# Eighteen convolution taps a layer moved from VectorE to ScalarE products and accumulating transfers, and VectorE's remaining taps placed anew

## The chip, the cores and the metric

The kernel runs on one core of a Trainium2 chip. The metric is the device time of one execution in microseconds. The kernel before takes 1769.1 us, the median of three runs (1768.19 to 1769.87).

## What is computed

The reference is a trunk of two layers (sequence 512, width 1024). Each layer feeds three mixers with one projection of the normed input, gates them per channel, and goes on to a feed-forward and an embedding:

```python
h = rmsnorm(x, norm_mix[i])
qa, ka, va, glu_in, qc, kc, vc, gates = jnp.split(h @ w_in[i], SPLITS, axis=-1)
ya = diff_attention(qa, ka, va, ...)          # 4 heads, two softmaxes a head
yb = conformer_conv(glu_in, ...)              # the part that the change touches
yc = neighbourhood_attention(qc, kc, vc, rpb) # 8 heads on an 8 x 64 grid
ga, gb, gc = jnp.split(jax.nn.sigmoid(gates), 3, axis=-1)
merged = ga * (ya @ w_br_a) + gb * (yb @ w_br_b) + gc * (yc @ w_br_c)
x = x + merged @ w_o[i]
...                                           # feed-forward, gated embedding
```

The convolution module is a gated unit `z = a * sigmoid(g)`, then a depthwise convolution over the sequence with 31 taps for each of 512 channels, a bias, a layer norm and a silu. A depthwise tap is a product of a shifted row with one number per channel, and a sum.

## The kernel before

**Engines.** All matrix products are on TensorE (PE), in pairs of high and low parts: each weight block of 128x1024 is loaded by SyncE's queue (SP) into a tile `wr`, ScalarE (ACT) copies it to `wh`, VectorE (DVE) subtracts to get `wl` (`split`, called by `weights`, lines 166 to 177). Activations are split in the same way. PE's order is the order of the program text; the other engines' instructions are placed by a scheduler from priorities and dependencies.

**Order of a layer** (`layer`, from line 432). Names in the profile begin with the stage: `glu` (three of the four blocks of the gated unit), `natten` (neighbourhood attention: `natten_in` for queries and keys of two heads at a time, `natten_v` for the values, whose four sums stand in PSUM as two `natten_mm`, a `natten_av` and a `natten_sc`), the last gated block, `diff` (differential attention: `diff_in` for each of four heads, `diff_v` for the values) with `gatec` (eight blocks of gate c, one after `diff_in(1)`, seven after `diff_in(3)`), `gateb`, `branchc`, `mergea`, more `gateb`, the convolution's norm (`conv`), `mergeb`, `wo`, the feed-forward `ffn`, and `ple`. Attention units (scores, softmax, values) are generators; a counter of PE's chunks starts them some chunks after their inputs, and runs their later steps, so that they lie between the blocks of other stages.

**Softmax steps that the prediction uses.** In a neighbourhood unit PE writes scores to a PSUM tile `natten_sc` (L722; two buffers, shared with the value sum of that name and with `diff_sc`), VectorE takes the minimum (L726), ScalarE the exponential. In a differential unit VectorE takes the maximum (L919), ScalarE writes the exponentials `diff_a` and `diff_e`. At the end of a head ScalarE scales the output (`diff_t`), GpSimd (POOL) raises the mean square to a power (`diff_rc`, L227, inside `norm`), and PE transposes that column (`diff_tr`, L231).

**The taps.** 31 taps for each of four filters j (128 channels each) are steps of VectorE over the whole sequence, 124 a layer: the first a product plus bias (L549), the others a product plus the sum so far (L164, `conv_z<-glu_z,pre_par,conv_z`). They are one generator, `taps`, drawn in order of j and then of tap by `background(act, n)`: it takes the next n taps and lets each follow a given step of the stage. A table of numbers, `BG` (line 49), says how many a step of each stage draws; what is left at the norm is drawn there (`conv`).

**Tiles.** `z` has 5 buffers (gated inputs and sums), `t` has 7 (temporary tiles of 128x512 for all stages), `b` has 2 (biases of neighbourhood units, later quarters of the feed-forward's activations).

**GpSimd** has little else in this part of the program: the power steps, and from the output projection on the feed-forward's accumulating transfers (L1004, `ffn_qk<-w_fu`: it issues a DMA that adds what it brings to what is in the tile).

Of the kernel before, what the change touches and what calls it, by code (L numbers as in the profile page):

```python
# [14 lines left out]
AF = mybir.ActivationFunctionType  # L15
ALU = mybir.AluOpType
# [4 lines left out]
P = 128  # L21
# [3 lines left out]
GR = 8  # L25
# [5 lines left out]
CON3W = 31  # L31
# [14 lines left out]
PAR_L = 8 + 8 + 8 + 1 + 4 + 4 + 4 + 4 * CON3W  # L46
PAR = L * PAR_L + 8
WARM = 8
BG = dict(glu=2, natten=1, values=3, diff=1, gatec=2, branchc=2, gateb=4, mergea=4, mergea2=2)
FIRST = (["v"] * 4 + ["pt"] * 2 + ["y", "b"], ["y"] * 5 + ["pt"] * 2 + ["b"])  # L50
EARLY = 6
QUARTERS = (2, 4, 6)
# [13 lines left out]
class Net:  # L66
# [229 lines left out]
    def build(self):  # L296
        nc, tc, a = self.nc, self.tc, self.a
        self.bufs = dict(wr=3, wh=3, wl=3, h=8, qk=2, kh=2, v=4, pt=2, y=5, z=5, x=4, t=7, rp=4,
                         e=4, a=3, r=2, rb=1, ss=1, sm=8, rc=4, b=2, s=8)
        self.bg, self.w_ahead = BG, 400  # L300
        self.pbufs = dict(mm=3, sc=2, tr=2, av=1)
# [130 lines left out]
    def layer(self, i, h, xsrc, xs):  # L432
        self.i, self.h = i, h
        zs, cs = [], []
        self.todo = self.taps(zs, cs)
        self.glu(zs)
        if i == 0:
            self.lambdas()
        yc, ya, yb = [], [], []
        sn, sd = {}, {}  # L440
        self.natten_in(0, sn, yc)
        self.drain(self.renorm)
        self.h = self.hs
        self.natten_v(sn)
        last = self.glu_last(zs)
        self.natten_in(1, sn, yc)
        next(last)
        self.natten_in(2, sn, yc)
        next(last)
        self.natten_in(3, sn, yc)  # L450
        acc, gb = [], []
        self.diff_in(0, sd, ya)
        self.diff_v(0, sd)
        self.diff_in(1, sd, ya)
        self.gate_c(acc, 0)
        self.diff_in(2, sd, ya)
        self.diff_v(1, sd)
        self.diff_in(3, sd, ya)
        for m in range(1, KD):
            self.gate_c(acc, m)  # L460
        for m in range(2):
            self.gate_b(gb, m, AF.Copy, None)
        for g in acc + gb:
            self.act(g, g, AF.Sigmoid, table="sigmoid")
        self.branch_c(acc, yc)
        for m in range(2, 4):
            self.gate_b(gb, m, AF.Sigmoid, "sigmoid")
        self.merge_a(ya, acc)
        conv = self.run(self.conv(cs, yb))
        pairs = self.inputs()  # L470
        for m in range(4, KD):
            self.gate_b(gb, m, AF.Sigmoid, "sigmoid")
            for n in ((0, 1), (2,), (3,), ())[m - 4]:
                self.input_block(pairs, n)
        self.drain(conv)
        mg = self.merge_b(yb, acc, gb)
        ws = self.pair_weights(4)
        x, h = self.w_o(mg, xsrc)
        self.input_pair(ws, pairs, 4)
        h = self.ffn(h, x)  # L480
        return self.ple(h, x, xs, self.inputs())
# [57 lines left out]
    def taps(self, zs, cs):  # L539

        for j, z in enumerate(zs):
            zf = z.rearrange("p a b -> p (a b)")
            c = self.sb("z", [P, 512])
            cs.append(c)
            for d in range(CON3W):
                w = self.par(self.i, "cw", j * CON3W + d)
                src = zf[:, d * GR:d * GR + 512]
                if d == 0:
                    yield self.nc.vector.tensor_scalar(c, src, w, self.par(self.i, "cb", j),  # L549
                                                       ALU.mult, ALU.add)  # L550
                else:
                    yield self.stt(c, src, w, c, ALU.mult, ALU.add)

    def background(self, after, n):

        ph, self.phase = self.phase, "conv"
        for _ in range(n):
            i = next(self.todo, None)
            if i is not None:
                self.tc.add_manual_dep(  # L560
                    i.ins, after.ins.name,
                    mybir.DependencyInfo(mybir.DependencyClass.NoSync, mybir.DependencyReason.DATA),
                    reason="background")
        self.phase = ph
# [214 lines left out]
    def gate_c(self, acc, m):  # L779
        self.phase = "gatec"  # L780
        ps = self.proj(OFF_G + 2 * D + m * P)
        if m % 2 == 0:
            acc += self.parts_of("x", [512], 2)
        self.background(self.act(acc[m], ps, AF.Copy), self.bg["gatec"])

    def branch_c(self, acc, ys):
        self.phase = "branchc"
        for m in range(KD):
            ps = self.ps("mm")
            self.gemm(ps, self.a["w_br_c"][self.i, m], ys)  # L790
            self.background(self.tt(acc[m], acc[m], ps, ALU.mult), self.bg["branchc"])
# [692 lines left out]
```

## Time and profile before

| | before |
|---|---|
| median of three runs | 1769.1 us |
| profiled execution, first to last instruction (span) | 1766.6 us |
| mean granted TensorE clock | 1.000 |
| DMA, mean over the span | 144 GB/s |
| VectorE's taps but the first ones (L164, `conv_z`), both layers | 240 x 748 ns |
| layer 0, 43 to 97 us (neighbourhood values, first units): VectorE busy | 45.69 of 54.00 us |
| layer 0, 165 to 300 us (differential attention, gate c): ScalarE busy | 75.28 of 135.00 us |

The profile is of one execution; the page gives its span and no other time of it. Layer 1 repeats layer 0's stages some 875 us later. Rows of a timeline read: start, duration, engine, line, operation, written tile<-read tiles, shapes, count, and in brackets the idle time ahead with what ended it. Rows of groups read: line, engine, operation, names, shapes, count | busy us, mean ns of one | idle before and its causes. Rows of one line's instructions give the count, then the shortest, median and longest duration in ns, and the first and last start. Rows of waits read: who waited <- for whom: total us, times, longest.

### The profile page before, as it was taken

The page shows a single profiled execution, that of the slowest core. Times are in us where ns is not written, and L with a number is a line of the kernel's source. Part 1 is how long each engine was busy: PE and PEld are TensorE (multiplying, and loading weights), DVE is VectorE, ACT ScalarE, POOL GpSimd, SP SyncE. Part 2 cuts the span into 40 slices and gives each one's busy share as a digit, 9 for nine tenths or more (in the row PEclk, how much of TensorE's full clock was granted, in tenths as well). Part 3 has the DMA queues.
Part 4 walks back from the last instruction along what each step waited for, and adds up shares of the span by engine and source line. Part 5 has one row for each costly group of instructions (what it writes and reads, how often), then busy time and mean ns, then how long its engine had stood idle before and what let it go on. Part 6 is the DMA issues. An engine that isn't in the chain of part 4 may idle for free.

```text
span 1766.6 us, 27127 instructions
## 1 busy us (share of the span) xinstructions
PE 1759.3 (100%) x10146; PEld 1551.8 (88%) x10146; DVE 1408.6 (80%) x2354; ACT 885.5 (50%) x1529; POOL 98.4 (6%) x114
## 2 busy tenths in 40 slices
PE   9999999999999999999999999999999999999998
PEld 7888888888899899998888888888888998989987
DVE  7967988998898587787777688889887976867776
ACT  5576555325565254454545655552356643534444
POOL 0000000000111010100000000000001110101000
PEclk9999999999999999999999999999999999999999
DMA  6575641334757365544446655322356674655332
GB/s 231 158 186 160 162 123 54 102 100 150 222 153 196 106 173 156 137 126 127 151 137 173 180 148 154 108 73 94 101 183 194 168 179 118 172 141 156 99 104 96
DMA packets 112548, 253.95 MB, mean 144 GB/s; under 512 B 14368, under 2 KB 23328, under 8 KB 112416
## 3 DMA queue, kind: packets, MB, share of 16 engines
q1 hardware_dynamic: 99024, 227.83, 42.0%
q0 software_dynamic: 12672, 23.07, 8.1%
q8 instruction: 80, 1.31, 0.3%
q10 hardware_dynamic: 720, 1.31, 0.2%
q14 instruction: 52, 0.43, 0.1%
HBM read 214.41 MB, written 7.34 MB: 126 GB/s over the span
## 4 chain that ended last, share of the span: by engine, by line
PE 92%; DVE 4%; DMA 2%; ACT 2%; issue 1%; SPq 0%; POOL 0%; ACTq 0%; POOLq 0%; DVEq 0%
PE ffn_mm L1034 4%; PE ffn_mm L1036 4%; PE ffn_mm L182 4%; PE ffn_mm L181 4%; PE ffn_mm L183 4%; PE ffn_mm L1035 4%; PE ffn_sc L1036 3%; PE ffn_sc L1034 3%; PE ffn_sc L1035 3%; PE mergea_mm L182 2%; PE mergea_mm L183 2%; PE mergea_mm L181 2%; PE gateb_mm L182 2%; PE gateb_mm L183 2%; PE gateb_mm L181 2%; PE wo_mm L182 2%
## 5 line engine op out<-in xcount | busy, mean ns | idle before, releaser
L164 DVE SCALAR_TENSOR_TENSOR conv_z<-glu_z,pre_par,conv_z 128x512 f32<-128x512 f32 x240 | 179.6, 748 | 3.5
L147 ACT ACTIVATE ffn_wh<-ffn_wr 128x1024 fp32r<-128x1024 f32 (+1 forms) x92 | 92.8, 1015 | 111.9 <-PE ffn_mm L182 81.4
L1004 POOL DMA_DIRECT2D ffn_qk<-w_fu x88 | 78.1, 978 | 605.6 <-DMA ffn_qk<-w_fu 289.7
L161 DVE TENSOR_TENSOR ffn_wl<-ffn_wr,ffn_wh 128x1024 fp32r<-128x1024 f32 (+1 forms) x92 | 107.4, 1173 | 5.3 <-ACT ffn_wh L147 4.6
L161 DVE TENSOR_TENSOR ffn_t<-ffn_mm,wo_rb 128x512 f32<-128x512 f32 (+1 forms) x64 | 38.7, 605 | 68.4 <-PE ffn_mm L183 68.4
L147 ACT ACTIVATE mergea_wh<-mergea_wr 128x1024 fp32r<-128x1024 f32 (+1 forms) x32 | 27.1, 848 | 96.8 <-PE mergea_mm L182 79.5
L147 ACT ACTIVATE ffn_wh<-ffn_qk 128x1024 fp32r<-128x1024 f32 x44 | 46.7, 1061 | 37.1 <-PE ffn_mm L182 15.9
L161 DVE TENSOR_TENSOR ffn_wl<-ffn_qk,ffn_wh 128x1024 fp32r<-128x1024 f32 x44 | 53.9, 1224 | 10.7 <-ACT ffn_wh L147 10.7
L161 DVE TENSOR_TENSOR ffn_t<-ffn_t,ffn_t 128x512 f32<-128x512 f32 (+1 forms) x46 | 31.3, 680 | 31.9 <-ACT ffn_t L147 31.4
L147 ACT ACTIVATE natten_e<-natten_e,natten_s 128x192 f32<-128x192 f32 (+1 forms) x88 | 39.3, 474 | 25.2 <-DVE natten_s L726 21.9
L181 PE MATMUL ffn_mm<-ffn_v,ffn_wh 128*128 128x512 f32 x132 | 51.4, 389 | 0.0
L182 PE MATMUL ffn_mm<-ffn_v,ffn_wh 128*128 128x512 f32 x132 | 51.4, 389 | 0.0
L183 PE MATMUL ffn_mm<-ffn_v,ffn_wl 128*128 128x512 f32 x132 | 51.3, 389 | 0.0
L181 PE MATMUL ffn_mm<-ffn_y,ffn_wh 128*128 128x512 f32 x132 | 51.3, 389 | 0.0
L182 PE MATMUL ffn_mm<-ffn_y,ffn_wh 128*128 128x512 f32 x132 | 51.3, 389 | 0.0
L183 PE MATMUL ffn_mm<-ffn_y,ffn_wl 128*128 128x512 f32 x132 | 51.3, 389 | 0.0
L147 ACT ACTIVATE diff_a<-diff_sc,diff_s 128x512 f32<-128x512 f32 x32 | 22.0, 687 | 57.1 <-DVE diff_s L919 57.0
L1036 PE MATMUL ffn_mm<-wo_h,ffn_wl 128*128 128x256 f32 x176 | 49.8, 283 | 0.0
L1036 PE MATMUL ffn_sc<-wo_h,ffn_wl 128*128 128x256 f32 x176 | 49.8, 283 | 0.0
L1035 PE MATMUL ffn_sc<-wo_h,ffn_wh 128*128 128x256 f32 x176 | 49.8, 283 | 0.0
L1035 PE MATMUL ffn_mm<-wo_h,ffn_wh 128*128 128x256 f32 x176 | 49.8, 283 | 0.0
L1034 PE MATMUL ffn_sc<-wo_h,ffn_wh 128*128 128x256 f32 x176 | 49.8, 283 | 0.0
(879 smaller groups left out, 6539.8 us busy)
## 6 DMA issues: line engine op xcount, KB each, us to landing
ffn_qk<-w_fu POOLq DMA_DIRECT2D x88, 256.0 KB, 5.7
ffn_wr<-w_fg SPq DMA_DIRECT2D x44, 512.0 KB, 3.7
ffn_wr<-w_fd SPq DMA_DIRECT2D x32, 448.0 KB, 4.1
ffn_r<-w_fu SPq DMA_DIRECT2D x44, 256.0 KB, 4.2
ffn_qk<-w_fg SPq DMA_DIRECT2D x44, 256.0 KB, 4.0
ffn_qk<-w_fu SPq DMA_DIRECT2D x44, 256.0 KB, 4.2
natten_wr<-w_in SPq DMA_DIRECT2D x16, 512.0 KB, 4.3
diff_wr<-w_in SPq DMA_DIRECT2D x16, 512.0 KB, 4.2
```

Source lines behind the costliest of these rows:

```text
L147: i = self.nc.scalar.activation(out, in_, func, **kw)
L161: return self.nc.vector.tensor_tensor(out, a, b, op)
L164: return self.nc.vector.scalar_tensor_tensor(out, a, s, b, op0, op1)
L181: mm(out, wh, ah, start=first, stop=False)
L182: mm(out, wh, al, start=False, stop=False)
L183: mm(out, wl, ah, start=False, stop=last)
L1004: nc.gpsimd.dma_start(q, wu[:, lo], accum_op=ALU.add)
L1034: mm(out, wh[:, c], bh, start=first and k == 0, stop=False, skip_group_check=True)
L1035: mm(out, wh[:, c], bl, start=False, stop=False, skip_group_check=True)
L1036: mm(out, wl[:, c], bh, start=False, stop=k == 3, skip_group_check=True)
```

## The change

Taps 0 to 8 of filters 2 and 3 leave VectorE, 18 a layer. A generator `chain` makes them, alternating between the two filters, into two tiles `self.far` of tag `b`. Tap 0 is one ScalarE step with scale and bias straight into the tile. Each later one is a ScalarE product into a temporary tile of tag `t`, then a DMA that GpSimd issues and that adds this tile to `far`. `link` draws one of them. Every block of gate c draws two, and there is one more behind each of `diff_in(2)` and `diff_in(3)`: 18 in all. VectorE's taps of filters 2 and 3 then begin at tap 9 and work on `far`. Taps drawn per step change in four stages: neighbourhood values 3 to 4, gate b 4 to 2, merge a 4 to 3 and 2 to 1.

```diff
-BG = dict(glu=2, natten=1, values=3, diff=1, gatec=2, branchc=2, gateb=4, mergea=4, mergea2=2)
+BG = dict(glu=2, natten=1, values=4, diff=1, gatec=2, branchc=2, gateb=2, mergea=3, mergea2=1)
+LINKS = 18
...
-        self.todo = self.taps(zs, cs)
+        self.todo, self.links = self.taps(zs, cs), self.chain(zs)
...
         self.diff_in(2, sd, ya)
+        self.link()
         self.diff_v(1, sd)
         self.diff_in(3, sd, ya)
+        self.link()
...
-            c = self.sb("z", [P, 512])
+            if j < 2:
+                c, n = self.sb("z", [P, 512]), 0
+            else:
+                for _ in self.links:
+                    pass
+                c, n = self.far[j - 2], LINKS // 2
             cs.append(c)
-            for d in range(CON3W):
+            for d in range(n, CON3W):
...
+    def chain(self, zs):
+        self.far = [self.sb("b", [P, 512]) for _ in range(2)]
+        for n in range(LINKS):
+            d, j = divmod(n, 2)
+            w = self.par(self.i, "cw", (j + 2) * CON3W + d)
+            src = zs[j + 2].rearrange("p a b -> p (a b)")[:, d * GR:d * GR + 512]
+            if d == 0:
+                self.act(self.far[j], src, AF.Identity, scale=w, bias=self.par(self.i, "cb", j + 2))
+            else:
+                t = self.sb("t", [P, 512])
+                self.act(t, src, AF.Copy, scale=w)
+                self.nc.gpsimd.dma_start(self.far[j], t, accum_op=ALU.add)
+            yield
+
+    def link(self):
+        ph, self.phase = self.phase, "conv"
+        next(self.links, None)
+        self.phase = ph
...
         self.background(self.act(acc[m], ps, AF.Copy), self.bg["gatec"])
+        self.link()
+        self.link()
```

PE's instructions are the same in number and order. Lines of the changed kernel stand one lower in the file up to `layer` (L148 is ScalarE's step, L162 and L165 VectorE's two, L228 the power step), and by about thirty more after the new functions (L755 for the minimum, L1035 for the feed-forward's transfers); L574 is the new transfer. Numbers at the ends of names count tiles and differ by a few.

**VectorE, layer 0, while the neighbourhood values' PSUM is emptied**, before (x, v: parts of the values; wl: weight splits):

```order
L161 TENSOR_TENSOR glu_wl_840<-glu_wr_838,glu_wh_839 128x1024
L161 TENSOR_TENSOR natten_v_697<-natten_mm_561,natten_v_697 64x4x128
L161 TENSOR_TENSOR natten_v_699<-natten_sc_564,natten_v_699 64x4x128
L161 TENSOR_TENSOR natten_v_698<-natten_mm_562,natten_v_698 64x4x128
L161 TENSOR_TENSOR natten_v_698<-natten_av_563,natten_v_698 64x4x128
L161 TENSOR_TENSOR natten_x_701<-natten_sc_564,natten_x_701 64x4x128
L161 TENSOR_TENSOR natten_wl_921<-natten_wr_919,natten_wh_920 128x1024
L161 TENSOR_TENSOR natten_v_699<-natten_av_563,natten_v_699 64x4x128
```

and at the same place now:

```order
L162 TENSOR_TENSOR glu_wl_844<-glu_wr_842,glu_wh_843 128x1024
L165 SCALAR_TENSOR_TENSOR conv_z_370<-glu_z_321,pre_par_67,conv_z_370 128x512
L162 TENSOR_TENSOR natten_v_701<-natten_mm_561,natten_v_701 64x4x128
L165 SCALAR_TENSOR_TENSOR conv_z_370<-glu_z_321,pre_par_67,conv_z_370 128x512
L162 TENSOR_TENSOR natten_v_703<-natten_sc_564,natten_v_703 64x4x128
L165 SCALAR_TENSOR_TENSOR conv_z_370<-glu_z_321,pre_par_67,conv_z_370 128x512
L162 TENSOR_TENSOR natten_v_702<-natten_mm_562,natten_v_702 64x4x128
L162 TENSOR_TENSOR natten_wl_925<-natten_wr_923,natten_wh_924 128x1024
L165 SCALAR_TENSOR_TENSOR conv_z_370<-glu_z_321,pre_par_67,conv_z_370 128x512
L162 TENSOR_TENSOR natten_x_705<-natten_sc_564,natten_x_705 64x4x128
L755 ISA natten_e_785,natten_s_789<-natten_sc_790,natten_e_785 128x192
```

Four taps and the weight split `natten_wl` stand ahead of `natten_x<-natten_sc`, and the two steps that read `natten_av` behind it.

**ScalarE, layer 0, between gate c's third block and the next attention unit**, before:

```order
L147 ACTIVATE gatec_x_2594<-gatec_mm_2529 128x512
L147 ACTIVATE diff_ss_2591<-diff_av_2427 128x512
L147 ACTIVATE diff_t_2590<-diff_av_2427,glu_subg_447 128x512
L147 ACTIVATE diff_e_2559,diff_s_2548<-diff_sc_2555,diff_s_2548 128x512
L147 ACTIVATE diff_a_2633,diff_sm_2090<-diff_sc_2629,diff_s_2628 128x512
L147 ACTIVATE diff_e_2639,diff_s_2628<-diff_sc_2635,diff_s_2628 128x512
```

and now (`conv_t` are the products):

```order
L148 ACTIVATE gatec_x_2614<-gatec_mm_2549 128x512
L148 ACTIVATE diff_ss_2611<-diff_av_2438 128x512
L148 ACTIVATE diff_t_2610<-diff_av_2438,glu_subg_447 128x512
L148 ACTIVATE diff_e_2579,diff_s_2568<-diff_sc_2575,diff_s_2568 128x512
L148 ACTIVATE conv_t_2618<-glu_z_327,pre_par_67 128x512
L148 ACTIVATE conv_t_2621<-glu_z_840,pre_par_67 128x512
L148 ACTIVATE conv_t_2701<-glu_z_327,pre_par_67 128x512
L148 ACTIVATE conv_t_2704<-glu_z_840,pre_par_67 128x512
L148 ACTIVATE conv_t_2780<-glu_z_327,pre_par_67 128x512
L148 ACTIVATE conv_t_2783<-glu_z_840,pre_par_67 128x512
L148 ACTIVATE diff_a_2659,diff_sm_2098<-diff_sc_2655,diff_s_2654 128x512
L148 ACTIVATE diff_e_2665,diff_s_2654<-diff_sc_2661,diff_s_2654 128x512
```

Six products stand in a row between the second exponential of one unit and the first of the next.

**GpSimd, layer 0**, before, all of its steps between the gated unit and the feed-forward:

```order
L227 TENSOR_TENSOR glu_rc_317<-glu_sm_315,pre_power_104 128x4
L227 TENSOR_TENSOR diff_rc_2307<-diff_sm_2305,pre_power_104 128x4
L227 TENSOR_TENSOR diff_rc_2626<-diff_sm_2624,pre_power_104 128x4
L227 TENSOR_TENSOR diff_rc_2911<-diff_sm_2909,pre_power_104 128x4
L227 TENSOR_TENSOR diff_rc_3187<-diff_sm_3185,pre_power_104 128x4
L227 TENSOR_TENSOR conv_rc_4005<-conv_sm_4003,pre_power_104 128x4
```

and now the last part of the same stretch (`conv_b` are the two tiles `far`):

```order
L574 DMA conv_b_1929<-conv_t_2852 128x512
L574 DMA conv_b_1930<-conv_t_2855 128x512
L574 DMA conv_b_1929<-conv_t_2927 128x512
L574 DMA conv_b_1930<-conv_t_2930 128x512
L574 DMA conv_b_1929<-conv_t_3010 128x512
L228 TENSOR_TENSOR diff_rc_2961<-diff_sm_2959,pre_power_104 128x4
L574 DMA conv_b_1930<-conv_t_3013 128x512
L228 TENSOR_TENSOR diff_rc_3239<-diff_sm_3237,pre_power_104 128x4
L228 TENSOR_TENSOR conv_rc_4037<-conv_sm_4035,pre_power_104 128x4
```

The third power step stands behind the last transfer but one, and the fourth behind the last.

## The prediction, made before the changed kernel ran

> **What bounds the kernel now.** I read the page's busy times first, then the chain that ended last, then the waits of TensorE (PE), and then the stretches that the change touches.
>
> ```profile
> span 1766.6 us, 27127 instructions
> PE 1759.3 (100%) x10146; PEld 1551.8 (88%) x10146; DVE 1408.6 (80%) x2354; ACT 885.5 (50%) x1529; POOL 98.4 (6%) x114
> PE 92%; DVE 4%; DMA 2%; ACT 2%; issue 1%; SPq 0%; POOL 0%; ACTq 0%; POOLq 0%; DVEq 0%
> ```
>
> PE is busy for all of the span and makes 92% of the chain. Its share alone would not prove much, since the ends of matmuls are modelled, so the waits decide:
>
> ```profile
> PE pre_av L329 <- DVE pre_zeror L402: 1.1, 1, 1.1
> PE natten_av L763 <- DVE natten_a L161: 0.3, 1, 0.3
> ```
>
> That is the whole list: 1.1 us before the program has data, and 0.3 us once. TensorE never stands still for a convolution tap, an exponential or a gate. VectorE's stretches say the same:
>
> ```profile
> 60.00:80.00 20.00, 20.00 (x91) 16.61 (x90) 19.33 (x26) 9.38 (x13) 0.00 (x0) 1.00 0.55 162
> 200.00:290.00 90.00, 90.00 (x495) 77.50 (x494) 75.08 (x134) 48.09 (x98) 3.04 (x3) 1.00 0.39 107
> 300.00:400.00 100.00, 100.00 (x453) 82.99 (x452) 91.60 (x129) 29.42 (x43) 1.43 (x1) 1.00 0.35 104
> ```
>
> Columns: length, then busy time and instructions of PE, weight loads, VectorE, ScalarE, GpSimd, then the granted clock (1.00), the DMA share and GB/s. The first stretch is layer 0's neighbourhood values, the second the attention units with gate c, the third branch c and merge a. VectorE is at 97%, 83% and 92% there, close to full, and PE still has no gap. So work taken from VectorE is worth only what PE waits for it, which is almost nothing; work put ahead of something that PE needs soon costs its full length.
>
> **What is removed.** Each layer loses 18 taps of 124 on VectorE: two first ones and sixteen others.
>
> ```profile
> L164 DVE SCALAR_TENSOR_TENSOR conv_z<-glu_z,pre_par,conv_z x240: 733/748/755, 37.7 to 1268.1; 128x512 f32<-128x512 f32 x120
> L549 DVE TENSOR_SCALAR conv_z<-glu_z,pre_par x8: 537/543/547, 36.7 to 1227.8; 128x512 f32<-128x512 f32 x8
> ```
>
> Over both layers that is 32 x 0.748 + 4 x 0.543 = 26.1 us of VectorE. They go from branch c, gate b and merge a, where the third stretch shows PE without a gap. Credited: 0. The most that a lighter VectorE could return is PE's own wait for it, 0.3 us in the list above (0.5 with the weight load in front of it).
>
> **What is moved, and the only term that I charge.** Taps per weight block of the neighbourhood values go from 3 to 4, so four more taps a layer stand among the steps that empty the value product's PSUM. In layer 0 VectorE did this before:
>
> ```profile
> 71.72 0.73 DVE L164 SCALAR_TENSOR_TENSOR conv_z<-glu_z,pre_par,conv_z 128x512 f32<-128x512 f32 x1
> ...
> 73.20 0.75 DVE L164 SCALAR_TENSOR_TENSOR conv_z<-glu_z,pre_par,conv_z 128x512 f32<-128x512 f32 x1
> 73.87 1.22 DVE L161 TENSOR_TENSOR glu_wl<-glu_wr,glu_wh 128x1024 fp32r<-128x1024 f32 x1
> ...
> 77.28 0.69 DVE L161 TENSOR_TENSOR natten_v<-natten_av,natten_v 64x512 fp32r<-64x512 f32 x1
> 78.00 0.70 DVE L161 TENSOR_TENSOR natten_x<-natten_sc,natten_x 64x512 fp32r<-64x512 f32 x1
> 78.73 1.23 DVE L161 TENSOR_TENSOR natten_wl<-natten_wr,natten_wh 128x1024 fp32r<-128x1024 f32 x1
> 79.87 0.69 DVE L161 TENSOR_TENSOR natten_v<-natten_av,natten_v 64x512 fp32r<-64x512 f32 x1
> ```
>
> and PE needed it here:
>
> ```profile
> 80.05 0.29 PE L722 MATMUL natten_sc<-natten_x,natten_qk 128*128 128x256 f32 x1
> 80.17 0.28 PE L722 MATMUL natten_sc<-natten_qk 128*128 128x256 f32 x1
> ```
>
> The natten_x step at 78.00 is the last reader of a PSUM buffer named natten_sc. There are two of these; the first unit's first half of scores takes the other, its second half (80.17) takes this one and waits for VectorE. It had 80.17 - 78.70 = 1.47 us to spare. In the changed order four taps and the weight split (78.73) stand ahead of natten_x, and one natten_v step goes behind it. A tap there occupies 0.67 us (73.20 to 73.87) to 0.76 us (71.72 to 72.48), the split 1.14 us (78.73 to 79.87), the natten_v step 0.72 us (77.28 to 78.00). So natten_x ends later by 4 x 0.67 + 1.14 - 0.72 = 3.1 us to 4 x 0.76 + 1.14 - 0.72 = 3.5 us; near the low end, since most of these taps precede no wait, I take 3.2. PE then stands 3.2 - 1.5 = **1.7 us**. Behind PE's wait nothing else gets later by as much: PE's own later needs shift with it. One wait goes under:
>
> ```profile
> 97.41 0.44 PE L763 MATMUL natten_av<-natten_a,natten_x 128*128 128x128 f32 x2 [0.31 <-DVE natten_a L161]
> PEld natten_av L763 <- DVE natten_a L161: 0.5, 1, 0.5
> ```
>
> A PE that arrives 1.7 us later finds natten_a ready if ScalarE's and VectorE's steps before it follow PE by less than that, which their order allows: -0.5. Net **+1.2 us**, between +0 (the steps pack closer) and +2.
>
> In layer 1 the four taps fall into a pause:
>
> ```profile
> 938.58 1.53 DVE L164 SCALAR_TENSOR_TENSOR conv_z<-glu_z,pre_par,conv_z 128x512 f32<-128x512 f32 x2
> 942.68 1.23 DVE L161 TENSOR_TENSOR natten_wl<-natten_wr,natten_wh 128x1024 fp32r<-128x1024 f32 x1 [2.57 <-ACT natten_wh L147]
> 945.61 0.68 DVE L161 TENSOR_TENSOR natten_x<-natten_mm,natten_x 64x512 fp32r<-64x512 f32 x1 [1.70 <-ACT natten_x L147]
> ```
>
> 4 x 0.76 = 3.0 us against idle 2.57 and then 1.70: used up before natten_x. 0.
>
> **What is added: 18 products a layer on ScalarE.** The row of one such copy (PSUM source) and of a group that holds one wait place:
>
> ```profile
> L147 ACT ACTIVATE gatec_x<-gatec_mm 128x512 f32<-128x512 f32 x8 | 4.7, 595 | 3.4 <-PE diff_sc L828 3.4
> L147 ACT ACTIVATE diff_a<-diff_sc,diff_s 128x512 f32<-128x512 f32 x16 | 11.0, 687 | 28.5 <-DVE diff_s L919 28.4
> 243.43 0.22 ACT L147 ACTIVATION_READ_ACCUMULATOR diff_e<-diff_sc,diff_s 128x1 f32 x1
> 246.55 0.69 ACT L147 ACTIVATE diff_a<-diff_sc,diff_s 128x512 f32<-128x512 f32 x1 [2.89 <-DVE diff_s L919]
> ...
> 254.29 0.69 ACT L147 ACTIVATE diff_a<-diff_sc,diff_s 128x512 f32<-128x512 f32 x1 [3.72 <-DVE diff_s L919]
> ```
>
> ScalarE waits 28.5 us before 16 exponentials; products fill that. The largest lump is six in a row after 243.65: 6 x 0.595 = 3.6 us against 2.89, so the next exponentials start at most 0.7 us late. The next such exponential follows 7.7 us later (254.29), after another pause of 3.72, so the lag is made up there. 0, and 0.7 a layer if that cover were gone.
>
> **What is added: 16 accumulating transfers a layer, issued by GpSimd.** No such transfer from SBUF stands in the trace; the nearest are the feed-forward's, from HBM in a busier stage:
>
> ```profile
> L1004 POOL DMA_DIRECT2D ffn_qk<-w_fu x88: 865/883/1247, 449.3 to 1635.3; - x88
> DMA to landing us min/median/max: 3.6/5.7/9.2
> 272.95 0.68 ACT L147 ACTIVATE diff_t<-diff_av,glu_subg 128x512 f32<-128x512 f32 x1
> 277.23 1.01 POOL L227 TENSOR_TENSOR diff_rc<-diff_sm,pre_power 128x4 f32<-128x4 f32 x1 [29.56 <-DVE diff_sm L164]
> 282.76 0.60 PE L231 MATMUL diff_tr<-pre_ident,diff_rc 128*128 128x128 f32 x4
> ```
>
> Each transfer waits for the one before into the same buffer, and GpSimd's queue waits with it. The third head's power step (277.23) now stands behind the third of the last four transfers. Their products follow diff_t, so the first of the four issues at about 272.95 + 0.68 + 0.6 = 274.2; the third goes to the same buffer, so it waits until the first has landed (X), is issued (0.9), and then the power step takes 1.0: it ends at 274.2 + X + 1.9. PE needs it at 282.5. X = 3.6 gives 279.7, 5.7 gives 281.8, 9.2 gives 285.3: bounds 0 to 2.8 us a layer for this link alone. The DMA share is 0.39 here, so I take X between 3.6 and 5.7: **0**, with under 1 us of cover at 5.7.
>
> **Sum.** 1766.6 + 1.7 - 0.5 = 1767.8 us of span. The page gives the span alone; the median of the runs, 1769.1, is 2.5 us more, which I carry over: **1770.3 us**. A kernel like this can be told from no change from about 0.2% on, 3.5 us.
>
> **Rivals.**
> *The transfers hold up GpSimd's queue* (slower). The chain of a buffer decides as well: issues at 244.3 (behind diff_e), then every X, so that the third last is issued at 244.3 + 5X and the power step ends 1.9 later. From X = 6.4 on PE waits. At 9.2 it ends at 292.2, 9.7 us late a layer: 1766.6 + 1.2 + 2 x 9.7 + 2.5 = 1789.7; at 7.0 it is 0.6 a layer. For it: 5.7 is close to 6.4. Against it: half the DMA load. Chance 0.1.
> *GpSimd cannot write its descriptors while VectorE works.* In rows: each issue would wait for the VectorE instruction under way, at most the 1.23 us of a weight split; two issues lie on the path, so 281.8 + 2.5 = 284.3, 1.8 us a layer, 1773.9. The rows above speak against it (883 ns an issue, 1247 at worst, beside a full VectorE). Chance 0.05. The Trainium skill, SBUF — State Buffer, section "SBUF: two separate sides", has this rule: a VectorE instruction that uses both ports keeps GpSimd from writing descriptors, and it gives about 3.1 us instead of 0.6. The feed-forward's issues do not show it.
> *Nothing is moved in time, or VectorE's relief shows* (no change or faster). If the four taps pack into pauses, layer 0 loses nothing, and without the 0.5: 1768.6. Chance 0.17.
> *Something small in ScalarE's order* (exponentials, the shared temporary buffers, of which links hold up to seven): 2 to 5 us. Chance 0.08.
>
> **Chances and range.** The forecast has 0.6 (1769.3 to 1772). Faster by over 0.2% needs 3.5 us, and PE waits for less than that: 0.04. Slower by over 0.2%: the upper part of the first rival, the second and half of the last, 0.19. Within: 0.77. The range takes in no change below, less the 0.9 us by which the runs shown fall short of their median and a little of PE's own wait, and the second rival above: 1767.0 to 1775.
>
> **What would show it.** Right: PE's waits name natten_sc behind natten_x once, near 80 us, with 1.5 to 2 us, nothing at 955; the natten_a wait is gone; power steps end before 282.5; accumulate landings of 3.6 to 5.7 us. Wrong: a PE wait on diff_rc or on diff_tr, landings over 6.4 us, or a PE wait in the mergea or gateb stretch.

## The result, and the profile after

The changed kernel takes 1775.64 us (median of five runs, 1772.76 to 1775.99) against 1768.65 us for the kernel before: ratio 1.0034, 95% interval 1.0022 to 1.0046. It is slower by 6 to 7 us. A second measurement beside the last experiments gave 1774.75 us and 1.0037 (1.0024 to 1.0049). The first time lies 0.6 us above the top of the stated range (1775), the second just below it; neither is near the forecast (1770.3). A slowdown of over 0.2% had been given a chance of 0.19. The profiled execution has a span of 1773.7 us, 7.1 more than before.

The profile page's first lines, and then the list of PE's waits:

```profile
span 1773.7 us, 27221 instructions
PE 1761.2 (99%) x10146; PEld 1552.9 (88%) x10146; DVE 1383.8 (78%) x2318; ACT 906.4 (51%) x1565; POOL 127.5 (7%) x146
```

```profile
PE diff_mm L182 <- DVE natten_y L162: 3.1, 2, 2.2
PE natten_sc L751 <- DVE natten_x L162: 1.7, 1, 1.7
PE pre_av L330 <- DVE pre_zeror L403: 1.1, 1, 1.1
PE diff_tr L232 <- DVE diff_pt L162: 0.9, 1, 0.9
```

VectorE has lost 24.8 us of work (1408.6 to 1383.8; the sum of the taps had given 26.1), and PE waits more than before. Three waits are new; natten_a's 0.3 us is gone.

**The natten_sc wait** is the forecast one. VectorE's last reader of the buffer, and PE's second half of scores:

```profile
81.09 0.69 DVE L162 TENSOR_TENSOR natten_x<-natten_sc,natten_x 64x512 fp32r<-64x512 f32 x1
```
```profile
81.94 0.36 PE L751 MATMUL natten_sc<-natten_qk 128*128 128x256 f32 x1 [1.70 <-DVE natten_x L162]
```

natten_x starts at 81.09 instead of 78.00, 3.1 us later (forecast 3.2), and PE stands 1.70 us (forecast 1.7). The last tenth of that is luck: PE starts 0.16 us after natten_x has ended (81.78), a handing over that the forecast's 1.47 us to spare had counted as free, and the shorter delay makes up for it.

**The diff_mm wait** was not forecast at all. First the same place before the change, VectorE, SyncE's queue and PE, which the prediction never looked at. The rows `diff_rp<-diff_rp` of SyncE are the rotations that the rope needs: 64 KB copies within SBUF that swap blocks of 32 partitions.

```profile
150.18 0.69 DVE L161 TENSOR_TENSOR diff_rp<-diff_rp,diff_r 128x512 f32<-128x512 f32 x1 [0.69 <-DMA diff_rp<-diff_rp]
...
156.18 0.68 DVE L161 TENSOR_TENSOR natten_y<-natten_y,natten_mm 64x512 fp32r<-64x512 f32 x1
```
```profile
144.59 1.77 SPq L846 DMA_DIRECT2D diff_rp<-diff_rp  x3
```
```profile
157.01 0.47 PE L181 MATMUL diff_mm<-glu_h,diff_wh 128*128 128x512 f32 x1
```

VectorE waits 0.69 us for the last rotation, and six microseconds of steps queue behind it in order; the last of them, natten_y, frees the PSUM buffer that PE's next block takes. It ends at 156.18 + 0.68 = 156.86, and PE starts at 157.01. The 0.15 us between them is no slack: where PE does wait for this step, below, it starts just as long after it (160.87 and 161.01). So nothing was to spare here. Now the same in the changed kernel, with GpSimd's row first:

```profile
145.91 1.05 POOL L574 DMA_DIRECT2D conv_b<-conv_t  x1 [116.58 <-ACT conv_b L148]
```
```profile
145.79 1.77 SPq L877 DMA_DIRECT2D diff_rp<-diff_rp  x3
```
```profile
154.19 0.69 DVE L162 TENSOR_TENSOR diff_rp<-diff_rp,diff_r 128x512 f32<-128x512 f32 x1 [4.00 <-DMA diff_rp<-diff_rp]
...
160.19 0.68 DVE L162 TENSOR_TENSOR natten_y<-natten_y,natten_mm 64x512 fp32r<-64x512 f32 x1
```

The first accumulating transfer stands far ahead of its place in the text: the scheduler put its product among the last neighbourhood units, where everything it needs was there. It starts together with the last three rotations of the first head. From the start of their issue to VectorE's step it is now 8.4 us (145.79 to 154.19), before 5.6 (144.59 to 150.18). PE waits 2.22 us, and then its matmuls start 0.43 us apart instead of 0.23. The last row below is a stretch of time, with the columns that the prediction names. Its granted clock is 0.50; from 156 to 161 us it was 1.00.

```profile
161.01 0.47 PE L182 MATMUL diff_mm<-glu_h,diff_wh 128*128 128x512 f32 x1 [2.22 <-DVE natten_y L162]
161.32 0.40 PE L183 MATMUL diff_mm<-glu_h,diff_wh 128*128 128x512 f32 x1
161.56 0.39 PE L184 MATMUL diff_mm<-glu_h,diff_wl 128*128 128x512 f32 x1
161.79 0.56 PE L182 MATMUL diff_mm<-glu_h,diff_wh 128*128 128x512 f32 x1
162.15 0.63 PE L183 MATMUL diff_mm<-glu_h,diff_wh 128*128 128x512 f32 x1
162.58 0.63 PE L184 MATMUL diff_mm<-glu_h,diff_wl 128*128 128x512 f32 x1
163.00 0.63 PE L182 MATMUL diff_mm<-glu_h,diff_wh 128*128 128x512 f32 x1
```
```profile
162.00:165.00 3.00, 3.00 (x8) 2.32 (x8) 2.58 (x9) 2.07 (x6) 0.00 (x0) 0.50 0.85 199
```

Eight of them do so, eight times 0.2 us: 1.6 us more. Of the 3.1 us in the list, the other 0.9 is the same wait in layer 1. **The diff_tr wait** of 0.9 us is in layer 1 too. The sum: 3.1 + 1.7 + 0.9 - 0.3 + 1.6 = 7.0 of the 7.1 us.

The landing of the 32 transfers, from the rows of their line:

```profile
L574 POOL DMA_DIRECT2D conv_b<-conv_t x32: 859/880/1162, 145.9 to 1162.8; - x32
DMA to landing us min/median/max: 3.2/4.6/8.3
```

The feared 6.4 us is passed by some of them (the first takes 8.3 us, the one at 1100 us 8.0, and three pairs issued together have medians of 6.6 and 6.7), but the last four of layer 0, for which it was feared, have a median of 3.7 us, and no PE wait names a power step of GpSimd.

### The profile page after: what moved, and what is told of

The parts are those of the page before. It is cut to its first block, busy times and chain, and to the rows that moved or that the text cites. A ratio compares the mean times of both kernels' runs of the same rounds, so it can differ in the third digit from the quotient of the medians.

```text
span 1773.7 us, 27221 instructions
## 1 busy us (share of the span) xinstructions
PE 1761.2 (99%) x10146; PEld 1552.9 (88%) x10146; DVE 1383.8 (78%) x2318; ACT 906.4 (51%) x1565; POOL 127.5 (7%) x146
## 4 chain that ended last, share of the span: by engine, by line
PE 94%; DVE 3%; DMA 1%; ACT 1%; issue 1%; SPq 0%; POOL 0%; ACTq 0%; POOLq 0%; DVEq 0%
PE ffn_mm L1065 4%; PE ffn_mm L1067 4%; PE ffn_mm L183 4%; PE ffn_mm L182 4%; PE ffn_mm L184 4%; PE ffn_mm L1066 4%; PE ffn_sc L1067 3%; PE ffn_sc L1065 3%; PE ffn_sc L1066 3%; PE mergea_mm L183 2%; PE mergea_mm L184 2%; PE mergea_mm L182 2%; PE gateb_mm L183 2%; PE gateb_mm L184 2%; PE gateb_mm L182 2%; PE wo_mm L183 2%
## 5 line engine op out<-in xcount | busy, mean ns | idle before, releaser
L148 ACT ACTIVATE ffn_wh<-ffn_wr 128x1024 fp32r<-128x1024 f32 (+1 forms) x92 | 92.7, 1014 | 111.7 <-PE ffn_mm L183 81.2
L1035 POOL DMA_DIRECT2D ffn_qk<-w_fu x88 | 77.8, 981 | 605.6 <-DMA ffn_qk<-w_fu 289.7
L162 DVE TENSOR_TENSOR ffn_wl<-ffn_wr,ffn_wh 128x1024 fp32r<-128x1024 f32 (+1 forms) x92 | 107.4, 1173 | 5.4 <-ACT ffn_wh L148 4.9
L162 DVE TENSOR_TENSOR ffn_t<-ffn_mm,wo_rb 128x512 f32<-128x512 f32 (+1 forms) x64 | 38.7, 605 | 68.2 <-PE ffn_mm L184 68.2
L165 DVE SCALAR_TENSOR_TENSOR conv_z<-glu_z,pre_par,conv_z 128x512 f32<-128x512 f32 x120 | 89.7, 747 | 1.3
L148 ACT ACTIVATE mergea_wh<-mergea_wr 128x1024 fp32r<-128x1024 f32 (+1 forms) x32 | 27.1, 846 | 96.8 <-PE mergea_mm L183 79.6
L165 DVE SCALAR_TENSOR_TENSOR conv_b<-glu_z,pre_par,conv_b 128x512 f32<-128x512 f32 x88 | 65.9, 749 | 1.3
L148 ACT ACTIVATE ffn_wh<-ffn_qk 128x1024 fp32r<-128x1024 f32 x44 | 46.7, 1061 | 37.2 <-PE ffn_mm L183 16.0
L574 POOL DMA_DIRECT2D conv_b<-conv_t x32 | 28.5, 939 | 489.7 <-ACT conv_b L148 244.9
L162 DVE TENSOR_TENSOR ffn_wl<-ffn_qk,ffn_wh 128x1024 fp32r<-128x1024 f32 x44 | 53.8, 1224 | 10.8 <-ACT ffn_wh L148 10.8
L162 DVE TENSOR_TENSOR ffn_t<-ffn_t,ffn_t 128x512 f32<-128x512 f32 (+1 forms) x46 | 31.3, 680 | 31.9 <-ACT ffn_t L148 31.4
L162 DVE TENSOR_TENSOR mergea_wl<-mergea_wr,mergea_wh 128x1024 fp32r<-128x1024 f32 (+1 forms) x32 | 30.7, 960 | 30.0 <-ACT mergea_wh L148 28.6
L148 ACT ACTIVATE natten_e<-natten_e,natten_s 128x192 f32<-128x192 f32 (+1 forms) x88 | 39.2, 473 | 29.0 <-DVE natten_s L755 26.0
L1066 PE MATMUL ffn_sc<-wo_h,ffn_wh 128*128 128x256 f32 x176 | 49.8, 283 | 0.0
```

The lines of the kernel that those rows point to most:

```text
L148: i = self.nc.scalar.activation(out, in_, func, **kw)
L162: return self.nc.vector.tensor_tensor(out, a, b, op)
L165: return self.nc.vector.scalar_tensor_tensor(out, a, s, b, op0, op1)
L574: self.nc.gpsimd.dma_start(self.far[j], t, accum_op=ALU.add)
L1035: nc.gpsimd.dma_start(q, wu[:, lo], accum_op=ALU.add)
L1066: mm(out, wh[:, c], bl, start=False, stop=False, skip_group_check=True)
```

## The experiments

Three theories stood after this. *Separate stalls*: value taps 1.4 us net, the first transfer beside the rotations 2.2 + 1.6 us and its twin in layer 1 0.9 us, the six products in a row 0.9 us. *Knock-on*: the natten stall makes everything behind it late. *ScalarE*: the products, not the transfers, delay the rotations.

### The values back to three taps

```diff
-BG = dict(..., values=4, ..., gateb=2, mergea=3, mergea2=1)
+BG = dict(..., values=3, ..., gateb=2, mergea=3, mergea2=1)
```

> The changed kernel with three taps per weight block of the neighbourhood values again (the four taps a layer go to later steps). Theory: the changed kernel's 7 us are three separate stalls: the value taps (1.7 us of PE at natten_sc, less 0.5 at natten_a), the first accumulating transfer beside the rope rotations (2.4 us of PE at diff_mm plus 1.6 us of slowed matmuls in layer 0, 0.9 in layer 1), six products in a row (0.9 in layer 1). Then this kernel loses 1.2 to 1.4 us against the changed one, about 1774.3, and diff_mm still waits 2 us. Rival: the natten stall pushes everything behind it late, diff_mm too: then the diff_mm waits go as well and the time is 1769 to 1770.

1779.36 us, ratio 1.0066 (1.0052 to 1.008): 10.5 us over the kernel before, where 5 to 6 were expected. PE's waits:

```profile
PE conv_tr L608 <- ACT conv_rp L148: 2.9, 2, 1.4
PE diff_mm L182 <- DVE natten_y L162: 1.8, 2, 1.2
PE conv_tr L609 <- DVE conv_rp L162: 1.7, 2, 0.8
PE diff_tr L232 <- DVE diff_pt L162: 1.4, 2, 1.0
```

The natten_sc wait is gone and the diff_mm wait stays, which speaks against knock-on. But a wait that neither theory had comes: the convolution's norm (conv_tr), 4.6 us over both layers. The four taps a layer have no place before the norm any more. By the table's numbers and the blocks of each stage, the changed kernel draws 4 (glu) + 8 (natten) + 16 (values) + 8 (diff) + 16 (gate c) + 16 (branch c) + 8 (four blocks of gate b) + 32 (merge a) = 108 taps ahead of the norm, for 106 to be done. Two are to spare; with three per weight block two are missing, and those ahead of them come late.

### The new spread without links

```diff
-        self.link()
-        self.link()
...
+            c, n = self.sb("z", [P, 512]), 0
```

(All links are gone; the taps of all four filters begin at 0 on VectorE.)

> The new spread of VectorE's taps, but no products and no transfers: all 124 taps on VectorE. Theory: the only stall left of the three is the one at natten_sc, 1.7 us, less 0.5 at natten_a: 1769.9 to 1770.1. Rival (the diff_mm wait follows from the natten stall or from VectorE's order, not from the transfers): diff_mm waits 2 us here as well, 1774. Second rival: the fewer taps drawn in gate b and merge a pile up before the convolution's norm, and PE waits there: over 1772.

1801.67 us, ratio 1.0185 (1.0171 to 1.0199). The second rival came, far larger than it was put:

```profile
PE conv_tr L601 <- ACT conv_rp L148: 25.9, 2, 13.0
PE natten_sc L744 <- DVE natten_x L162: 1.7, 1, 1.7
```

By the count above 124 - 108 = 16 taps a layer now have no place ahead of the norm, 12.0 us at 0.748; in layer 0 twelve of them stand in a row on VectorE from 404.17 to 413.58 us, while PE waits from 402 to 415. The two waits and natten_sc make 27.6 of the 32.8 us; behind the waits the granted clock is 0.50 (in 416 to 418 us, for example), and PE is busy for 5.0 us longer than before (1764.3 against 1759.3). So the relief by the links is real and is spent on the spread: fewer taps in gate b and merge a. And without transfers no diff_mm wait is in the list, although the natten stall is: knock-on falls.

### All products held at their place in the text

```diff
-        next(self.links, None)
+        after = self.last          # the ScalarE step made last
+        i = next(self.links, None)
+        ...                        # i is kept behind `after` on ScalarE
```

> Each product is kept behind the ScalarE step that stands before it in the program text, so no transfer starts before gate c's first block, and no six products stand in a row. Theory: the diff_mm waits (3.1 us and 1.6 us of slow matmuls) and the diff_tr wait (0.9) go; the natten_sc wait stays: 1769.8 to 1770.5. Rival: the transfers, 4 to 8 us each, meet the rotations of the third and fourth head instead, and a new diff_mm or diff_sc wait of 1 to 2 us comes: 1771 to 1773.

1780.1 us, ratio 1.0061 (1.0048 to 1.0074): worse. The diff_mm wait shrinks to 0.7 us, and the prediction's first rival appears:

```profile
PE diff_tr L232 <- POOL diff_rc L228: 5.2, 2, 2.9
```
```profile
250.05 0.89 POOL L574 DMA_DIRECT2D conv_b<-conv_t  x1 [2.78 <-DMA conv_b<-conv_t]
252.38 0.87 POOL L574 DMA_DIRECT2D conv_b<-conv_t  x1 [1.45 <-DMA conv_b<-conv_t]
256.68 0.86 POOL L574 DMA_DIRECT2D conv_b<-conv_t  x1 [3.43 <-ACT conv_t L148]
257.24 1.45 POOL L228 TENSOR_TENSOR diff_rc<-diff_sm,pre_power 128x4 f32<-128x4 f32 x1
```

The second head's power step stands behind transfers whose products are now late; it ends at 258.69, and PE waits 2.23 us for it.

### The same transfers without adding

```diff
-                self.nc.gpsimd.dma_start(self.far[j], t, accum_op=ALU.add)
+                self.nc.gpsimd.dma_start(self.far[j], t)
```

> Same order and same bytes, but the transfers overwrite the tile instead of adding to it (so taps 0 to 8 of the two filters but the last are left out of the result). Theory that the adding makes the first transfer slow (8.3 us to landing) and the rotations late: landings fall to 3 to 5 us, the diff_mm wait of layer 0 falls below 1 us, 1771. Rival: any transfer of 256 KB at that place does it: landing over 7 us, diff_mm waits 2 us, 1775.6 as before.

1774.33 us, ratio 1.0032 (1.0019 to 1.0045), not to be told from the changed kernel. Landings fall to 2.2/3.3/6.8 us (shortest, median, longest), but the first still takes 6.5 us, and PE's waits name diff_mm <- natten_y with 3.0 us in two times (1.6 the longest). The rival holds: a transfer beside the rotations does it, and the adding does not decide. (Its size was not varied.) What is absent here is the diff_tr wait of layer 1 and the slowed matmuls; the latter come and go between executions, as the last run shows.

### The products without the transfers

```diff
-                self.nc.gpsimd.dma_start(self.far[j], t, accum_op=ALU.add)
```

> The changed kernel with its ScalarE products but without the transfers (taps 1 to 8 of two filters are left out of the result). Theory: the transfers make the rope rotations land late, and so the diff_mm waits; without them those waits fall below 0.5 us in both layers, the natten_sc wait of 1.7 us stays, and the six products in a row cost 0 to 1 us a layer at diff_tr: 1769.5 to 1771. Rival: the products on ScalarE delay the softmax and the rotations; then diff_mm waits 1 to 2 us as with the transfers: 1774.

1771.05 us, ratio 1.0011 (1.0002 to 1.002). PE's whole list:

```profile
PE natten_sc L750 <- DVE natten_x L162: 1.7, 1, 1.7
PE pre_av L330 <- DVE pre_zeror L403: 1.1, 1, 1.1
```

The rotations of the place above need 5.4 us (before 5.6). All 36 products, six in a row in both layers, cost nothing (the 2.0 us over the kernel before are what the value taps take by themselves, below): the ScalarE theory falls, and so does my reading of the diff_tr wait as a price of the six alone. Each against the kernel before of its own session, the changed kernel loses 7.0 us (6.1 in the second measurement) and this one 2.0: the transfers cost 4 to 5 us.

### Links with the spread of before

```diff
-BG = dict(..., values=4, ..., gateb=2, mergea=3, mergea2=1)
+BG = dict(..., values=3, ..., gateb=4, mergea=4, mergea2=2)
```

> Products and transfers as in the changed kernel, but the taps drawn per step as before the change (values 3, gate b 4, merge a 4 and 2; the 106 taps then run out early). Theory: only the cost of the transfers is left, the changed kernel's 7 us less 1.4 at natten_sc: 1773 to 1775, no wait at conv_tr. Rival: the transfers were harmless and the spread did it: 1769.

1772.46 us, ratio 1.002 (1.0011 to 1.0028): 3.5 us slower than before, from 1773 to 1775 expected. The waits: diff_mm <- natten_y 1.4 us, diff_tr 1.0, diff_mm <- diff_v 0.8. No conv_tr wait, no natten_sc wait. The last of the three can't be charged to the transfers: it starts near 1056 us, and the version with the value taps alone, which has no transfers, shows it there with 0.6.

### Only the first three links held

The edit of the held version, for gate c's first block and the link behind `diff_in(2)` only.

> Only the first three links of a layer are kept behind the ScalarE step ahead of them in the text, so the first transfer starts some 40 us later, after the rotations of the first two heads; the others are placed by the scheduler as in the changed kernel. Theory: the diff_mm waits near 158 and 1037 us fall below 0.7 us and the slow matmuls behind them go; natten_sc keeps 1.7 us; up to 1 us a layer at diff_tr: 1770 to 1772. Rival: the delayed chain makes a power step of GpSimd late, as when all links were held (2.9 and 2.3 us at diff_tr): 1775 to 1777.

1772.29 us, ratio 1.0018 (1.0009 to 1.0027), just above the 1770 to 1772 expected. The first transfer starts at 213.5 us. As the theory had it, diff_mm waits 0.3 us in place of 3.1; diff_tr waits 0.8 us in each layer, named diff_pt, not the power step.

### The same, with three taps at the values and three at gate b

```diff
-BG = dict(..., values=4, ..., gateb=2, mergea=3, mergea2=1)
+BG = dict(..., values=3, ..., gateb=3, mergea=3, mergea2=1)
```

> As the one before, and the neighbourhood values draw three taps again, gate b three instead of two, so that all 106 taps are drawn ahead of the convolution's norm. Theory: neither the natten_sc wait (1.7) nor the conv_tr wait (2.7 a layer with values 3 and gate b 2) is there, natten_a's 0.5 is back: 1.4 us less than the one before, 1768.7 to 1771. Rival: the late last taps still hold the norm's products: conv_tr waits over 1 us a layer, 1772 or more.

1771.03 us, ratio 1.0008 (0.9999 to 1.0017): not told from the kernel before, nominally 2 us behind it. Neither natten_sc nor conv_tr waits. diff_mm still waits 0.9 us in layer 0, without a transfer near: the rotations took 6.7 us there, for a reason that stays open. It is the best of the versions with links, and no gain.

### The value taps alone, on the kernel before

```diff
-BG = dict(glu=2, natten=1, values=3, ...
+BG = dict(glu=2, natten=1, values=4, ...
```

> The kernel before, with one number changed: four taps per weight block of the neighbourhood values instead of three. Theory (the prediction's one charged term): PE waits 1.7 us at natten_sc near 80 us, the 0.3 us at natten_a go, nothing in layer 1: 1770.2 to 1770.5. Rival: the four taps that are drawn earlier relieve later stages, and the time is that of before, 1769.0; or the stall shifts more behind it than itself: over 1771.

1770.92 us, ratio 1.0013 (1.0004 to 1.0021), +2.3 us; its profiled execution took 1770.1, +1.5.

```profile
PE natten_sc L722 <- DVE natten_x L161: 1.7, 1, 1.7
PE pre_av L329 <- DVE pre_zeror L402: 1.1, 1, 1.1
PE diff_mm L181 <- DVE diff_v L161: 0.6, 1, 0.6
```

The charged term stands by itself: 1.7 us, natten_a gone. The 0.6 us at diff_mm, in layer 1, was in no forecast: VectorE waits there for the second head's rotations.

### One transfer beside the rotations

```diff
-LINKS = 18
+LINKS = 4
```

(with the spread of before; two first taps and two transfers a layer)

> Four links a layer instead of 18 (two first taps, two transfers), the spread of taps as before the change. The first transfer again starts near 145 us, beside the rotations, the second near 215 us; nothing else of the chain is there. Theory: the one transfer near 145 us (and its twin near 1024) is enough for a diff_mm wait of 1 to 2.4 us in layer 0: 1770 to 1772. Rival: one transfer does nothing by itself, and the time is 1769; then the diff_mm waits came from the chain as a whole or from chance.

1772.29 us, ratio 1.0023 (1.0014 to 1.0032), +3.7 us, as much as 16 transfers with the same spread (+3.5).

```profile
PE diff_mm L182 <- DVE natten_y L162: 2.8, 2, 2.2
PE pre_av L330 <- DVE pre_zeror L403: 1.1, 1, 1.1
PE natten_av L792 <- DVE natten_a L162: 0.3, 1, 0.3
```
```profile
145.26 1.05 POOL L574 DMA_DIRECT2D conv_b<-conv_t  x1 [115.25 <-ACT conv_b L148]
```

A single transfer a layer at this place is enough: the rotations take 8.2 us (here the trace puts VectorE's wait down to a later copy of SyncE's queue, `diff_qk<-diff_rp`). From the start of issue of the last three rotations to VectorE's step it is 5.3, 5.4, 5.4 and 5.6 us in the four kernels without transfers (before among them), 6.8, 6.8, 6.9, 7.1, 8.2 and 8.4 in the six with one beside the rotations, and 6.1, 6.4 and 6.7 in the three whose first transfer starts 67 us later. What delays the last three by about 1 us stays open; it wasn't tried. In layer 1 the two groups part cleanly: 6.0 to 7.4 us in the six kernels with a transfer beside the rotations, 4.9 to 5.7 in the other seven.

The Trainium skill, DMA: Bandwidth & Descriptors, section "Issuing engines are not separate DMA queues", says that transfers which ScalarE, SyncE or GpSimd start end up on the same 16 DMA engines and interleave. The pair of 8.2 us with one transfer and 5.6 before agrees: a transfer that GpSimd issued made SyncE's rotations late.

### The changed kernel once more

> The changed kernel itself once more, beside the two others. Theory: 5 to 7.5 us over the kernel before, with the same three places of waiting; slow matmuls behind the diff_mm wait where that is over 2 us. Rival: the first measurement had a bad draw of the rotations' landing, and the changed kernel is only 3 to 4 us slower, like the one with the old spread.

1774.75 us, ratio 1.0037 (1.0024 to 1.0049), +6.1 us: the theory's side. In its profiled execution the slow matmuls stand behind the natten_sc wait instead (83.3 to 86.6 us), and diff_mm waits 1.9 us in two times.

## Why the prediction was right and wrong

**What bounds it: right.** PE had hardly anything to wait for, and 25 us less on VectorE gave nothing back. The relief, credited with 0, did have a use that the prediction did not see: it pays for the thinner spread in gate b and merge a. Without it the spread costs 13 us a layer.

**The value taps: right,** in place and size: natten_x later by 3.1 us, PE's wait 1.70, natten_a's wait gone, nothing in layer 1. The sum of +1.2 us is what the traces give for it alone (+1.5 in the profiled execution); the median gives +2.3. The 0.6 us wait at diff_mm in layer 1 may be part of the rest; whether the value taps cause it is not shown.

**The transfers: wrong.** The step that failed is "0" for the 16 accumulating transfers, with only GpSimd's queue as their risk. That rival's mechanism exists (the version with all products held shows it, 5.2 us), but in the changed kernel the chain was early enough. The price came from a thing that was left out: what a transfer does to other transfers, 4 to 5 us. I took the chain's start from the text, at gate c, and looked at its lumps after 243 us; the first one starts at 145.91, beside the first head's rotations, and I did not look at who moves data there. Nor did I look for places where PE has no slack: natten_y, which ends just in time, stood in the trace of before. Two of the signs of being wrong that the prediction names did show, a wait on diff_tr and landings over 6.4 us, but neither by the way it meant: the wait is on VectorE, not on a power step. That the range came near the time is luck: its top had been set by another mishap, GpSimd kept from writing descriptors (1773.9), and the issues show none (859 to 1162 ns; the feed-forward's, before, 865 to 1247).

**The six products: right that they cost nothing by themselves,** wrong in what covers them. Layer 1's diff_tr wait is 0.9 us with the accumulating transfers and absent with the products alone and with plain copies. ScalarE's exponential ahead of the six, and the products, in layer 0 and then in layer 1 of the changed kernel; PE's transposes behind that exponential's unit, and the late ones, in the same two layers:

```profile
248.19 0.70 ACT L148 ACTIVATE diff_e<-diff_sc,diff_s 128x512 f32<-128x512 f32 x1
...
1124.95 0.70 ACT L148 ACTIVATE diff_e<-diff_sc,diff_s 128x512 f32<-128x512 f32 x1
...
1125.61 3.80 ACT L148 ACTIVATE conv_t<-glu_z,pre_par 128x512 f32<-128x512 f32 x6
```
```profile
249.24 0.60 PE L218 MATMUL diff_tr<-pre_ident,diff_ss 128*128 128x128 f32 x4
...
1125.06 0.60 PE L218 MATMUL diff_tr<-pre_ident,diff_ss 128*128 128x128 f32 x4
...
1133.87 0.62 PE L232 MATMUL diff_tr<-pre_ident,diff_rc 128*128 128x128 f32 x4 [0.91 <-DVE diff_pt L162]
```

ScalarE is 1.05 us ahead of PE in layer 0 (248.19 against 249.24) and 0.11 in layer 1: 0.9 us less cover, and PE waits 0.91. The prediction had sought the cover in ScalarE's pauses; it is this lead. The eight executions with six products in a row bear it out: in fourteen of their sixteen layers lead and wait add up to 0.9 to 1.1 us (0.58 and 0.42, 0.31 and 0.73, 1.06 and none with the products alone), and in the other two ScalarE comes after PE and the wait is 0.96. What made ScalarE late is argued, not shown: rotations of the third and fourth head beside further transfers.

**The sum.** Value taps +2.3 (alone), links with the old spread +3.5: 5.8 of the 6.1 to 7.0 us measured for both. The rest lies within the scatter, which is wider with the change (3.2 us between its five runs).

## What to carry to other kernels

A DMA that is added to take work off an engine is paid in other DMAs' landing. Before it is called free, look at what else is in flight where the scheduler really puts it, and find the steps behind those landings whose consumer has no slack; an engine without waits does not mean that its suppliers have time to spare. The distance from a step's end to its consumer's start is not yet slack: here 0.15 us of it was the handing over itself. A spread of fill-in work is a sum: count what must be drawn before a deadline against what is drawn.

## What was not expected of the hardware

A stall of PE can be followed by about 3 us at half the granted clock, 0.50 in the profile's rows in place of 1.00: 512-column matmuls start 0.43 us apart instead of 0.23, six to eight of them, 1.2 to 1.6 us lost. It came behind the 2.2 us waits of the changed kernel and of the version with one transfer, behind two of the eight waits of 1.7 us at natten_sc, behind the longest wait of the held version (2.9 us) and behind both 13 us waits; behind the 2.2 us wait shown for the held version it did not, and behind no wait under 1.7 us. So stalls of about 2 us differ from execution to execution in their price. The Trainium skill, TensorE: Matmul & The Clock Gate, section "HAM oscillation — how this bites in real kernels", gives 3.4 us of idle PE as the gap to avoid; here gaps of half to two thirds of that were sometimes enough, and the measurement decides.
